# Inverse roots in two VectorE steps, with the logarithm reading the raw sum, and a last row tile in 512, 256, 128 and 128 columns

## The chip, the cores and the metric

The kernel runs on one core of one Trainium2 chip. The metric is device time in microseconds of one execution; lower is better. The core has a matmul engine (TensorE, PE in the profile, its weight loads PEld), VectorE (DVE), ScalarE (ACT), GpSimd (POOL) and SyncE (SP), which here issues all the DMAs.

## The reference

Four layers on 512 tokens of width 1024, all in float32. Layers 0 and 1 have four branches each (latent attention, stick-breaking attention, attention with forget gates, memory attention), gated and merged, an output projection, and a layer norm of `alpha * x + out`. Layers 2 and 3 begin with an RMS norm, have four other attentions (dense, windowed, neighbourhood, difference), gates and an output projection onto the residual. A last RMS norm with its own gain gives the result. What matters here:

```python
def _layer_norm(x, g, b):
    mu = mean(x); var = mean(square(x - mu))
    return (x - mu) * rsqrt(var + 1e-5) * g + b

def _rmsnorm(x, g):
    return x * rsqrt(mean(x * x) + 1e-6) * g
```

Inside the attentions there are RMS norms as well: of the two latents, of the dense attention's queries and keys per head, and of the difference attention's outputs per head.

## The kernel before

Every product is made of three matmuls (`mm3`, L324 to 330): each float32 operand is split into a high and a low part, and high x high, high x low and low x high are summed in PSUM. Each matmul loads its own stationary operand, 128 x 128. The weights stream in as 128 x 1024 tiles and are split by ScalarE (L319) and VectorE (L322). Activations lie with features on partitions (`zth`, `ztl`).

Inside a layer the parts are generators, and a string of words written out by hand (`ORDER1`, `ORDER2`) sets the order in which they are called. When the program is built, the tile framework fixes each engine's own order and the semaphores from that; so on VectorE one finds operations of the next row tile between those of one norm. The engines then run their queues in order.

A layer ends in `w_out` (L1123 to 1145). It takes the 512 tokens in four row tiles of 128. For each tile it makes the output projection in column pieces of 512 (`fs`), in each piece 8 blocks of 3 matmuls (layers 0 and 1) or 6 blocks of 3 (layers 2 and 3, where two more blocks were multiplied earlier into `early`). The last row tile of the last layer is made in pieces of 512, 256 and 256 columns. After each piece VectorE adds the residual part (L1142 or L1144) into `y`. Then `post` (in `end`) takes the whole row tile:

- layers 0 and 1: `ln_rows` (L1171 to 1184): statistics by `bn_stats`, the variance plus epsilon (L1177), `y - mean` times gain for both halves (L1180), the inverse root, and the product with it plus the bias (L1184);
- layers 1, 2 and 3: `rms_rows` (L1156 to 1169): for each piece ScalarE squares it and sums it along the row (L1162, two records: the square and the read of its sum), VectorE multiplies by the gain (L1163) and adds the sum, scaled, to the previous one (L1165); then the inverse root; then the first 512 columns are scaled by VectorE (L1168) and the other 512 by ScalarE (L1169);
- except at the end, `to_feature` (L1147 to 1154) transposes the tile on PE (L1153) in two groups of four blocks of 128 columns, and splits it into `zth` and `ztl` for the next layer. At the end two DMAs of SyncE store the two halves (L1234).

The inverse root is `rsqrt` (L344 to 354). For a column `v` it forms exp(-ln(v)/2) on ScalarE (L348, L349) and one Newton step with four operations on VectorE (L350 to L353):

```python
nc.vector.tensor_tensor(t, y, y, ALU.mult)
nc.vector.tensor_tensor(t, t, v, ALU.mult)
nc.vector.tensor_scalar(t, t, -0.5, 1.5, ALU.mult, ALU.add)
nc.vector.tensor_tensor(y, y, t, ALU.mult)
```

It is called on one column by `ln_rows` and `rms_rows` (20 calls), on 8 columns by `mla` (2) and `diff_d` (4), and on 24 columns by `dense_a` (2).

Of the kernel before, what the change touches and what calls it, by code (L numbers as in the profile page):

```python
# [9 lines left out]
F32 = mybir.dt.float32  # L10
# [3 lines left out]
AF = mybir.ActivationFunctionType  # L14
ALU = mybir.AluOpType
# [4 lines left out]
DM = 1024  # L20
DEPTH = 2
ALPHA = (2 * DEPTH) ** 0.25
LN_EPS = 1e-5
RMS_EPS = 1e-6
# [264 lines left out]
def cols(i, n=128):  # L289
    return slice(n * i, n * i + n)  # L290
# [20 lines left out]
class Build:  # L311
# [29 lines left out]
    def small(self, n, name="sm"):  # L341
        return self.smp.tile([128, n], F32, tag=f"sm{n}", name=name, bufs=12 if n == 1 else 8 if n == 16 else 3)

    def rsqrt(self, v):  # L344

        nc, n = self.nc, v.shape[1]
        y, t = self.small(n, "rs_y"), self.small(n, "rs_t")
        nc.scalar.activation(y, v, AF.Ln)  # L348
        nc.scalar.activation(y, y, AF.Exp, scale=-0.5)  # L349
        nc.vector.tensor_tensor(t, y, y, ALU.mult)  # L350
        nc.vector.tensor_tensor(t, t, v, ALU.mult)
        nc.vector.tensor_scalar(t, t, -0.5, 1.5, ALU.mult, ALU.add)
        nc.vector.tensor_tensor(y, y, t, ALU.mult)  # L353
        return y


    def w_prefetch(self, upto):
# [304 lines left out]
    def setup(self):  # L662
        nc, tc, ctx = self.nc, self.tc, self.ctx
        pool = lambda n, b, **k: ctx.enter_context(tc.tile_pool(name=n, bufs=b, **k))
        self.cp = pool("const", 1)
        self.psp, self.pss, self.pst, self.pso = (pool(n, b, space=PSUM) for n, b in zip(("psp", "pss", "pst", "pso"), BANKS))
        self.rawp, self.wp = pool("raw", RAW), pool("wp", WP)
        self.smp = pool("small", 8)
        self.w_done, self.w_ready, self.wout, self.stp = 0, {}, None, None
        self.xs = [nc.dram_tensor(f"xs{i}", (S, DM), F32).ap() for i in range(3)]  # L670
        ct = self.cp.tile([128, NCONST], F32, name="ct")
        self.c = {k: ct[:, o : o + n] for k, (o, n) in COFF.items()}
        self.ident = self.c["ident"]
        big = lambda nm: self.cp.tile([128, 8, S], F32R, name=nm)
        self.zth, self.ztl = big("zth"), big("ztl")
        self.zp, self.z = pool("z", ZO), {}
        self.gated = set()
        nc.scalar.preload_act_table_set(EXPS)
        with tc.tile_pool(name="x0", bufs=1) as xp:
            x = xp.tile([128, 2, 8, 256], F32, name="x0")  # L680
            at = 0
            for n, (hf, k0, k1) in enumerate(X0):
                v = x[:, hf, k0:k1]
                c = slice(at, at + 256 * (k1 - k0))
                at = c.stop
                nc.sync.dma_start(v, self.ins["xt"][:, c].rearrange("p (k t) -> p k t", t=256))
                if n in W0:
                    self.w_prefetch(W0[n])
                self.split(*(t[:, k0:k1, cols(hf, 256)] for t in (self.zth, self.ztl)), v)
        self.w_prefetch(WP)  # L690
        nc.sync.dma_start(ct, self.ins["const"])
# [226 lines left out]
    def mla(self, l):  # L918
        nc = self.nc
# [24 lines left out]
                craw.append(c)  # L944
        v8 = self.small(8, "v8")
        v8v = v8.rearrange("p (a b) -> p a b", b=2)
        nc.vector.tensor_scalar(v8v[:, :, 0], stat[:, :, 0, 0], 1.0 / 384, RMS_EPS, ALU.mult, ALU.add)
        nc.vector.tensor_scalar(v8v[:, :, 1], stat[:, :, 1, 0], 1.0 / 256, RMS_EPS, ALU.mult, ALU.add)
        rs = self.rsqrt(v8).rearrange("p (a b) -> p a b", b=2)
        qsc = self.kp.tile([128, 4, 2], F32, tag="qsc", name="qsc")  # L950
        nc.vector.tensor_scalar(qsc[:, :, 0], rs[:, :, 0], 96.0**-0.5, None, ALU.mult)
# [171 lines left out]
    def w_out(self, kind, l, lhs, post, last):  # L1123
        nc = self.nc
        ks = range(len(lhs[0]))
        for k in ks:
            self.w_get((kind, l, k))
        woh, wol = self.wout
        for tt in range(4):
            c = cols(tt)  # L1130
            y = self.bp.tile([128, DM], F32, tag="y", name="y", bufs=2)
            rows = self.resid_rows.get(tt) or [y[:, f] for f in (cols(0, 512), cols(1, 512))]
            if kind == "wo" and tt not in self.resid_rows:
                nc.sync.dma_start(y, self.resid[c])
            fs = [cols(0, 512), cols(1, 512)]
            if last and tt == 3:
                fs[1:] = [cols(2, 256), cols(3, 256)]
            for f in fs:
                ps = self.pss.tile([128, S], F32, tag="S", name="pso")[:, : f.stop - f.start]
                self.mm3(ps, [(lhs[0][k][:, c], lhs[1][k][:, c], woh[:, k, f], wol[:, k, f]) for k in ks])  # L1140
                if kind == "wo":
                    nc.vector.scalar_tensor_tensor(y[:, f], rows[f.start // 512], ALPHA, ps, ALU.mult, ALU.add)  # L1142
                else:
                    nc.vector.tensor_tensor(y[:, f], self.early[tt][f.start // 512][:, f.start % 512 :][:, : f.stop - f.start], ps, ALU.add)  # L1144
            post(tt, y, fs)
# [10 lines left out]
    def rms_rows(self, y, g, out, fs):  # L1156

        nc = self.nc
        v = None
        for f in fs:  # L1160
            junk, ss = self.pso.tile([128, S], F32, tag="O", name="junk"), self.small(1, "ss")
            nc.scalar.activation(junk[:, : f.stop - f.start], y[:, f], AF.Square, accum_out=ss)  # L1162
            nc.vector.tensor_tensor(out[:, f], y[:, f], g[:, f], ALU.mult)  # L1163
            v2 = self.small(1, "ssv")
            nc.vector.tensor_scalar(v2, ss, 1.0 / DM, RMS_EPS if v is None else v, ALU.mult, ALU.add)  # L1165
            v = v2
        rs = self.rsqrt(v)
        nc.vector.tensor_scalar(out[:, cols(0, 512)], out[:, cols(0, 512)], rs, None, ALU.mult)  # L1168
        nc.scalar.activation(out[:, cols(1, 512)], out[:, cols(1, 512)], AF.Copy, scale=rs)  # L1169

    def ln_rows(self, y, g, b):  # L1171
        nc = self.nc
        st, mv, v = self.small(12, "bn"), self.small(2, "mv"), self.small(1, "var")
        for hf in range(2):
            nc.vector.bn_stats(st[:, cols(hf, 6)], y[:, cols(hf, 512)])
        nc.vector.bn_aggr(mv, st.rearrange("p (a b) -> p a b", b=6))
        nc.vector.tensor_scalar(v, mv[:, 1:2], LN_EPS, None, ALU.add)  # L1177
        for hf in range(2):
            f = cols(hf, 512)
            nc.vector.scalar_tensor_tensor(y[:, f], y[:, f], mv[:, 0:1], g[hf], ALU.subtract, ALU.mult)  # L1180
        rs = self.rsqrt(v)
        for hf in range(2):
            f = cols(hf, 512)
            nc.vector.scalar_tensor_tensor(y[:, f], y[:, f], rs, b[hf], ALU.mult, ALU.add)  # L1184
# [32 lines left out]
    def end(self, L, kind, lhs, last):  # L1217

        nc, l = self.nc, L % 2
        gn = self.row(6 if L == 3 else 3 + L, "rmsg") if L == 3 or L in (1, 2) and not last else None  # L1220

        def post(tt, y, fs):
            c = cols(tt)
            if L < 2:
                self.ln_rows(y, self.lng, self.lnb)
            if not last:
                nc.sync.dma_start(self.xs[L][c], y)
            if gn is not None:
                n = self.bp.tile([128, DM], F32, tag="n", name="n")
                self.rms_rows(y, gn, n, fs)  # L1230
                y = n
            if last:
                for f in (cols(0, 512), cols(1, 512)):
                    nc.sync.dma_start(self.out[c, f], y[:, f])  # L1234
            else:
                self.to_feature(tt, y)

        self.w_out(kind, l, lhs, post, last)
# [48 lines left out]
    def dense_a(self, l):  # L1287
# [9 lines left out]
            self.rope(r, cos, sin)  # L1297
            raw.append(r if t == 2 else self.q_stack(r))
        v = self.small(24, "va")
        nc.vector.tensor_scalar(v, stat.rearrange("p a b c -> p (a b c)"), 1.0 / 64, RMS_EPS, ALU.mult, ALU.add)  # L1300
        rs = self.rsqrt(v)
        rs4 = rs.rearrange("p (a b c) -> p a b c", b=3, c=2)
        qsc = self.kp.tile([128, 24], F32, tag="qsc", name="qsc")
# [57 lines left out]
    def diff_d(self, l):  # L1361
# [34 lines left out]
        for pr in range(2):  # L1396
            ku = [unit(hl[2], cols(2 * pr + c, 32), (0, 1, 0, 1)) for c in range(2)]
            o, sm = self.new_o(), self.sums()
            for e in range(2):
# [17 lines left out]
                if e:  # L1417
                    sq = self.tmp("sqd")
                    nc.scalar.activation(sq, o, AF.Square)
                    stat = self.pst.tile([128, 4, 1, 2], F32, tag="T", name="statd")  # L1420
                    self.head_sums(stat, 0, sq)

                    rc, v = self.recip(sm), self.sums()
                    nc.vector.tensor_tensor(v, rc, rc, ALU.mult)
                    nc.vector.scalar_tensor_tensor(v, v, 1.0 / 64, stat.rearrange("p a b c -> p (b c) a"), ALU.mult, ALU.mult)
                    nc.vector.tensor_scalar(v, v, RMS_EPS, None, ALU.add)
                    rs = self.rsqrt(v.rearrange("p a b -> p (a b)")).rearrange("p (a b) -> p a b", a=2)
                    nc.vector.tensor_tensor(rc, rc, rs, ALU.mult)
                    self.finish(6 + pr, o, rc, g)
# [65 lines left out]
```

## Time and profile before

| | us |
|---|---|
| median of 3 runs (lowest, highest) | 1360.04 (1359.38, 1360.09) |
| the profiled execution | 1360.33 |
| its span, first to last instruction | 1358.2 |
| TensorE busy | 1328.5 (98%) |
| VectorE busy | 1000.3 (74%) |
| ScalarE busy | 811.3 (60%) |

The profile is of one execution. Times in its rows count from the first instruction; the execution's own time is 2.1 us longer than the span. A row says when an operation started, how long it took, its engine and line, what it writes and reads, and its shape. Matmuls are pipelined, and a record of one overlaps the next, so what a matmul costs in a stream is read from start to start. In square brackets at the end of a row stands for how long the engine had stood still and what released it.

### The profile page before, as it was taken

To read this page: it belongs to the slowest core of one execution; us is meant where nothing else is said; L and a number is where in the kernel's file an instruction comes from. 1 tells how busy PE (TensorE), PEld (TensorE's weight loads), DVE (VectorE), ACT (ScalarE), POOL (GpSimd) and SP (SyncE) were. 2 spreads that over 40 slices of the span, in tenths; PEclk is the share of its full clock that TensorE was granted. 3 is DMA by queue.
4 is the path that set the end of the run, shared out by engine and by line. 5 is a ranking of instruction groups with operands and counts; after the bars stand their busy time and mean duration, and the time that the engine had idled before them with its cause. 6 is when DMAs were issued, how large, how long until landed. Compare 5 with 4: busy or idle time off the path is not lost.

```text
span 1358.2 us, 20047 instructions
## 1 busy us (share of the span) xinstructions
PE 1328.5 (98%) x7096; PEld 1096.4 (81%) x7096; DVE 1000.3 (74%) x2075; ACT 811.3 (60%) x1662; POOL 4.4 (0%) x12
## 2 busy tenths in 40 slices
PE   7999999999999999999999999999999999999997
PEld 7887788777789777877777898788887888888876
DVE  6567547898863677378989876789787576797875
ACT  4585556765413775467856344776875435778763
POOL 0000000000000000000000000000000000000000
PEclk9999999999999999999999999999999999999999
DMA  7543322343524443233236246323454265225521
GB/s 230 178 129 95 102 70 78 94 125 111 181 78 137 150 118 102 78 85 90 90 102 203 107 125 176 107 78 83 106 171 149 102 171 157 78 54 135 154 77 65
DMA packets 62419, 160.32 MB, mean 118 GB/s; under 512 B 11184, under 2 KB 11824, under 8 KB 62320
## 3 DMA queue, kind: packets, MB, share of 16 engines
q1 hardware_dynamic: 62320, 159.05, 39.6%
q8 instruction: 56, 0.92, 0.3%
q14 instruction: 43, 0.35, 0.1%
HBM read 117.92 MB, written 8.91 MB: 93 GB/s over the span
## 4 chain that ended last, share of the span: by engine, by line
PE 85%; DVE 6%; ACT 5%; issue 2%; DMA 2%; SPq 0%; DVEq 0%; ACTq 0%
PE proj L329 12%; PE proj L328 12%; PE proj L330 12%; PE T L551 4%; PE pso L330 3%; PE pso L328 3%; PE pso L329 3%; PE O L557 3%; PE O L558 2%; PE projwb L329 2%; PE projwb L330 2%; PE projwb L328 2%; PE s L512 2%; PE s L908 2%; PE projv L329 2%; PE projv L328 2%
## 5 line engine op out<-in xcount | busy, mean ns | idle before, releaser
L328 PE MATMUL proj<-zth,wh 128*128 128x512 f32 (+1 forms) x864 | 321.5, 373 | 6.9 <-ACT wh L319 5.6
L330 PE MATMUL proj<-zth,wl 128*128 128x512 f32 (+1 forms) x864 | 322.2, 373 | 0.0
L329 PE MATMUL proj<-ztl,wh 128*128 128x512 f32 (+1 forms) x864 | 321.7, 372 | 0.2
L322 DVE TENSOR_TENSOR wl<-raw,wh 128x1024 fp32r<-128x1024 f32 (+3 forms) x153 | 182.9, 1196 | 111.3 <-ACT wh L319 109.5
L319 ACT CAST wh<-raw 128x1024 fp32r<-128x1024 f32 (+3 forms) x153 | 157.9, 1032 | 138.2 <-PE proj L329 106.3
L328 PEld LDWEIGHTS proj<-zth,wh 128*128 128x128 f32 x864 | 163.5, 189 | 30.0 <-ACT wh L319 5.6
L329 PEld LDWEIGHTS proj<-ztl,wh 128*128 128x128 f32 x864 | 163.7, 189 | 23.6 <-DVE ztl L322 0.7
L330 PEld LDWEIGHTS proj<-zth,wl 128*128 128x128 f32 x864 | 163.5, 189 | 23.0 <-DVE wl L322 0.2
L322 DVE TENSOR_TENSOR tl<-T,th 128x512 fp32r<-128x512 f32 (+3 forms) x176 | 100.2, 576 | 23.2 <-ACT th L319 21.6
L319 ACT CAST th<-T 128x512 fp32r<-128x512 f32 (+3 forms) x176 | 86.6, 499 | 34.8 <-PE T L551 32.5
L551 PE MATMUL T<-ct,p 128*128 128x128 f32 x560 | 87.9, 274 | 2.0 <-DVE o L640 1.2
L528 DVE TENSOR_REDUCE nm<-s 128x1 f32<-128x512 f32 (+1 forms) x128 | 77.1, 612 | 11.1 <-PE s L1405 6.0
L551 PEld LDWEIGHTS T<-ct,p 128*128 128x128 f32 x560 | 67.7, 140 | 16.8 <-DVE o L640 2.9
L534 ACT ACTIVATE p<-s,nm 128x512 f32<-128x512 f32 (+1 forms) x96 | 59.4, 622 | 19.5 <-DVE nm L528 18.8
L557 PE MATMUL O<-tl,V 128*128 128x512 f32 (+3 forms) x160 | 59.2, 371 | 0.9 <-DVE tl L322 0.2
L558 PE MATMUL O<-th,V 128*128 128x512 f32 (+3 forms) x160 | 55.4, 350 | 0.0
L329 PE MATMUL projv<-wl,zth 128*128 128x256 f32 (+1 forms) x192 | 54.4, 283 | 0.0
L328 PE MATMUL projv<-wh,zth 128*128 128x256 f32 (+1 forms) x192 | 54.3, 283 | 0.0
L330 PE MATMUL projv<-wh,ztl 128*128 128x256 f32 (+1 forms) x192 | 54.3, 283 | 0.0
L329 PE MATMUL projwb<-y,wh 128*128 128x512 f32 x128 | 51.5, 403 | 0.0
L330 PE MATMUL projwb<-y,wl 128*128 128x512 f32 x128 | 50.9, 398 | 0.0
L328 PE MATMUL projwb<-y,wh 128*128 128x512 f32 x128 | 50.9, 398 | 0.0
(378 smaller groups left out, 2877.3 us busy)
## 6 DMA issues: line engine op xcount, KB each, us to landing
raw<-in_w_dram SPq DMA_DIRECT2D x173, 512.0 KB
xs<-y SPq DMA_DIRECT2D x12, 512.0 KB
ks<-hs SPq DMA_DIRECT2D x32, 128.0 KB
early<-xs SPq DMA_DIRECT2D x16, 256.0 KB
bias<-in_bias_dram SPq DMA_DIRECT2D x8, 448.0 KB
qs<-hs SPq DMA_DIRECT2D x24, 128.0 KB
qs<-ls SPq DMA_DIRECT2D x24, 128.0 KB
hs<-ls SPq DMA_DIRECT2D x24, 128.0 KB
```

What stands on the lines that cost most here:

```text
L319: self.nc.scalar.copy(h, src)
L322: self.nc.vector.tensor_tensor(l, src, h, ALU.subtract)
L328: self.nc.tensor.matmul(ps, ah, bh, start=i == 0, stop=False)
L329: self.nc.tensor.matmul(ps, ah, bl, start=False, stop=False)
L330: self.nc.tensor.matmul(ps, al, bh, start=False, stop=i == n - 1)
L512: self.nc.tensor.matmul(s, q[:, cols(i)], k[:, k0 : k0 + w], start=True, stop=False)
L528: nc.vector.tensor_reduce(nm, s, AX.X, ALU.max, negate=True)
L534: nc.scalar.activation(p[:, :w], src, AF.Exp, bias=nm, scale=sc, accum_out=sm)
L551: nc.tensor.transpose(T[:, cols(a)], P[i][:, c : c + 128], self.ident)
L557: nc.tensor.matmul(o, vsel(j), tl[:, :w], start=j == 0, stop=False, skip_group_check=True)
L558: nc.tensor.matmul(o, vsel(j), th[:, :w], start=False, stop=j == nk - 1, skip_group_check=True)
L908: nc.tensor.matmul(z[:, c:w], m, x, start=False, stop=n == len(sums) - 1, skip_group_check=True)
```

## The change

`rsqrt` now takes four times the mean (`v4`), and optionally the raw source with a scale and a bias that ScalarE applies inside the logarithm: w = exp(-ln(4v)/2) is half the inverse root, and the Newton step becomes (3 - w * v4 * w) * w. On one column that is two VectorE operations, on more columns three. All callers scale their means and epsilons by 4. `rms_rows` passes the last sum of squares as the source, with the running sum of the earlier pieces as a per-row bias; the scaled total `v` is still made on VectorE for the Newton step. `ln_rows` passes the variance as the source and a constant column with four times epsilon as the bias; that column is written once at the start. `rms_rows` scales columns 0 to 639 on VectorE and 640 to 1023 on ScalarE, and the two stores at the end are cut there too. The last row tile of the last layer is made in pieces of 512, 256, 128 and 128 columns.

```diff
-    def rsqrt(self, v):
-
-        nc, n = self.nc, v.shape[1]
-        y, t = self.small(n, "rs_y"), self.small(n, "rs_t")
-        nc.scalar.activation(y, v, AF.Ln)
-        nc.scalar.activation(y, y, AF.Exp, scale=-0.5)
-        nc.vector.tensor_tensor(t, y, y, ALU.mult)
-        nc.vector.tensor_tensor(t, t, v, ALU.mult)
-        nc.vector.tensor_scalar(t, t, -0.5, 1.5, ALU.mult, ALU.add)
-        nc.vector.tensor_tensor(y, y, t, ALU.mult)
-        return y
+    def rsqrt(self, v4, src=None, scale=1.0, bias=0.0):
+
+
+        nc, n = self.nc, v4.shape[1]
+        w, t = self.small(n, "rs_w"), self.small(n, "rs_t")
+        nc.scalar.activation(w, v4 if src is None else src, AF.Ln, scale=scale, bias=bias)
+        nc.scalar.activation(w, w, AF.Exp, scale=-0.5)
+        if n == 1:
+            nc.vector.scalar_tensor_tensor(t, w, v4, w, ALU.mult, ALU.mult)
+        else:
+            nc.vector.tensor_tensor(t, w, w, ALU.mult)
+            nc.vector.tensor_tensor(t, t, v4, ALU.mult)
+        nc.vector.scalar_tensor_tensor(w, t, 3.0, w, ALU.subtract, ALU.mult, reverse0=True)
+        return w
...
+        self.eps4 = self.cp.tile([128, 1], F32, name="eps4")
+        nc.vector.memset(self.eps4, 4 * LN_EPS)
...
             if last and tt == 3:
-                fs[1:] = [cols(2, 256), cols(3, 256)]
+                fs[1:] = [cols(2, 256), cols(6), cols(7)]
...
             v2 = self.small(1, "ssv")
-            nc.vector.tensor_scalar(v2, ss, 1.0 / DM, RMS_EPS if v is None else v, ALU.mult, ALU.add)
+            old = 4 * RMS_EPS if v is None else v
+            nc.vector.tensor_scalar(v2, ss, 4.0 / DM, old, ALU.mult, ALU.add)
             v = v2
-        rs = self.rsqrt(v)
-        nc.vector.tensor_scalar(out[:, cols(0, 512)], out[:, cols(0, 512)], rs, None, ALU.mult)
-        nc.scalar.activation(out[:, cols(1, 512)], out[:, cols(1, 512)], AF.Copy, scale=rs)
+        rs = self.rsqrt(v, ss, 4.0 / DM, old)
+        a, b = slice(0, 640), slice(640, DM)
+        nc.vector.tensor_scalar(out[:, a], out[:, a], rs, None, ALU.mult)
+        nc.scalar.activation(out[:, b], out[:, b], AF.Copy, scale=rs)
...
-        nc.vector.tensor_scalar(v, mv[:, 1:2], LN_EPS, None, ALU.add)
+        nc.vector.tensor_scalar(v, mv[:, 1:2], 4.0, 4 * LN_EPS, ALU.mult, ALU.add)
...
-        rs = self.rsqrt(v)
+        rs = self.rsqrt(v, mv[:, 1:2], 4.0, self.eps4)
...
             if last:
-                for f in (cols(0, 512), cols(1, 512)):
+                for f in (slice(0, 640), slice(640, DM)):
                     nc.sync.dma_start(self.out[c, f], y[:, f])
```

In `mla`, `dense_a` and `diff_d` the means are scaled by 4 (for instance `4.0 / 384, 4 * RMS_EPS` for `1.0 / 384, RMS_EPS`), and nothing else is changed there.

## Rows read from the trace of the kernel before

**Rows 1.** The page's busy times: engine, busy us, share, instructions.

```profile
PE 1328.5 (98%) x7096; PEld 1096.4 (81%) x7096; DVE 1000.3 (74%) x2075; ACT 811.3 (60%) x1662; POOL 4.4 (0%) x12
```

**Rows 2.** Timeline of the end: start us, duration us, engine, line, operation, tiles.

```profile
1351.34 0.28 PE L330 MATMUL pso<-wout,y 128*128 128x256 f32 x1
1351.65 0.42 DVE L1144 TENSOR_TENSOR y<-early,pso 128x256 f32<-128x256 f32 x1 [0.65 <-PE pso L330]
...
1352.17 0.39 ACT L1162 ACTIVATE junk<-y 128x256 f32<-128x256 f32 x1 [1.62 <-DVE y L1144]
1352.49 0.19 ACT L1162 ACTIVATION_READ_ACCUMULATOR junk<-y 128x1 f32 x1
...
1352.96 0.20 ACT L348 ACTIVATE rs_y<-ssv 128x1 f32<-128x1 f32 x1 [0.28 <-DVE ssv L1165]
...
1353.43 0.16 DVE L350 TENSOR_TENSOR rs_t<-rs_y 128x1 f32<-128x1 f32 x1 [0.50 <-ACT rs_y L349]
...
1354.20 0.72 ACT L1169 ACTIVATE n<-n,rs_y 128x512 f32<-128x512 f32 x1 [0.81 <-DVE rs_y L353]
1354.20 0.48 DVE L1168 TENSOR_SCALAR n<-n,rs_y 128x512 f32<-128x512 f32 x1
```

**Rows 3.** Timeline of PE, matmuls of 256 and of 128 columns (128x128).

```profile
1347.20 0.28 PE L328 MATMUL pso<-wout,y 128*128 128x256 f32 x1
1347.32 0.28 PE L329 MATMUL pso<-wout,y 128*128 128x256 f32 x1
...
254.96 0.27 PE L557 MATMUL O<-tl,V 128*128 128x128 f32 x1
255.07 0.28 PE L558 MATMUL O<-th,V 128*128 128x128 f32 x1
...
271.62 0.23 PE L557 MATMUL O<-tl,V 128*128 128x128 f32 x1
271.68 0.27 PE L558 MATMUL O<-th,V 128*128 128x128 f32 x1
...
132.77 0.44 PE L908 MATMUL s<-sp,tri 128*128 128x128 f32 x2 [0.65 <-DVE sp L322]
```

**Rows 4.** Groups by line and shape: count, busy us, mean ns, idle before.

```profile
L1144 DVE TENSOR_TENSOR y<-early,pso 128x256 f32<-128x256 f32 x2 | 0.8, 421 | 1.1 <-PE pso L330 1.1
L1162 ACT ACTIVATE junk<-y 128x512 f32<-128x512 f32 x7 | 4.2, 600 | 8.9 <-DVE y L1144 8.9
L1162 ACT ACTIVATE junk<-y 128x256 f32<-128x256 f32 x2 | 0.8, 388 | 2.8 <-DVE y L1144 2.8
L898 DVE SCALAR_TENSOR_TENSOR zt<-s,zt 128x128 f32<-128x128 f32 x8 | 2.2, 278 | 0.2
```

**Rows 5.** The same view: pairs without and with a scalar from memory.

```profile
L1296 ACT ACTIVATE qa<-proj,cols 128x512 f32<-128x512 f32 x1 | 0.7, 682 | 0.0
L1294 ACT ACTIVATE sq<-proj 128x512 f32<-128x512 f32 x1 | 0.6, 593 | 0.0
...
L1165 DVE TENSOR_SCALAR ssv<-ss,ssv 128x1 f32<-128x1 f32 x5 | 1.1, 211 | 1.2 <-ACT junk L1162 1.0
L1165 DVE TENSOR_SCALAR ssv<-ss 128x1 f32<-128x1 f32 x4 | 0.6, 150 | 1.6 <-ACT junk L1162 1.6
```

**Rows 6.** SyncE's second store; the DMAs' rate in slices of 0.1 us from 1354.2.

```profile
1355.14 0.38 SPq L1234 DMA_DIRECT2D out_dram<-n  x1
...
GB/s 0 0 0 0 0 0 0 0 0 0 0 0 0 143 389 471 389 369 410 389 451 369 369 430 471 369 205 21 0 0 0 0 0 0 0 0 0 0 0 0
```

**Rows 7.** Waits of PE, whole run: total us, times, longest us.

```profile
PE projn L328 <- DVE ml L985: 2.6, 2, 1.3
...
PE Tx L1153 <- DVE n L1168: 1.0, 3, 0.4
...
PE Tx L1153 <- issue: 0.4, 2, 0.3
PE Tx L1153 <- DVE y L1184: 0.4, 2, 0.2
```

More of the change, by code (lines that the diff above doesn't have):

```diff
@@ L946, in mla @@
         v8v = v8.rearrange("p (a b) -> p a b", b=2)
-        nc.vector.tensor_scalar(v8v[:, :, 0], stat[:, :, 0, 0], 1.0 / 384, RMS_EPS, ALU.mult, ALU.add)
-        nc.vector.tensor_scalar(v8v[:, :, 1], stat[:, :, 1, 0], 1.0 / 256, RMS_EPS, ALU.mult, ALU.add)
+        nc.vector.tensor_scalar(v8v[:, :, 0], stat[:, :, 0, 0], 4.0 / 384, 4 * RMS_EPS, ALU.mult, ALU.add)
+        nc.vector.tensor_scalar(v8v[:, :, 1], stat[:, :, 1, 0], 4.0 / 256, 4 * RMS_EPS, ALU.mult, ALU.add)
         rs = self.rsqrt(v8).rearrange("p (a b) -> p a b", b=2)
@@ L1299, in dense_a @@
         v = self.small(24, "va")
-        nc.vector.tensor_scalar(v, stat.rearrange("p a b c -> p (a b c)"), 1.0 / 64, RMS_EPS, ALU.mult, ALU.add)
+        nc.vector.tensor_scalar(v, stat.rearrange("p a b c -> p (a b c)"), 4.0 / 64, 4 * RMS_EPS, ALU.mult, ALU.add)
         rs = self.rsqrt(v)
@@ L1424, in diff_d @@
                     nc.vector.tensor_tensor(v, rc, rc, ALU.mult)
-                    nc.vector.scalar_tensor_tensor(v, v, 1.0 / 64, stat.rearrange("p a b c -> p (b c) a"), ALU.mult, ALU.mult)
-                    nc.vector.tensor_scalar(v, v, RMS_EPS, None, ALU.add)
+                    nc.vector.scalar_tensor_tensor(v, v, 4.0 / 64, stat.rearrange("p a b c -> p (b c) a"), ALU.mult, ALU.mult)
+                    nc.vector.tensor_scalar(v, v, 4 * RMS_EPS, None, ALU.add)
                     rs = self.rsqrt(v.rearrange("p a b -> p (a b)")).rearrange("p (a b) -> p a b", a=2)
```

## The prediction

> **What bounds the kernel now.** I read the page's busy times first, then the chain of work that ended last, then the timeline of the last microseconds, then TensorE's waits over the whole run. TensorE (PE) is busy for 1328.5 of 1358.2 us [rows 1], so before the very end an operation of another engine counts only where PE stands still for it. After PE's last matmul nothing else is left to run beside, and there every step counts in full. The reader should see in [rows 2] one dependent line: last matmul at 1351.34, addition of the early part, square, read of the sum, scaled sum (L1165), logarithm, exponential, four small operations (the first is L350), the two halves of the scaling at 1354.20. Two stores follow [rows 6]. From the addition at 1351.65 to the end of the span that is 6.55 us.
>
> **Change, part 1: 128-column pieces.** The last 256 columns of the last row tile become two pieces of 128. A piece is 6 blocks of rows times 3 products, 18 matmuls, and each loads its weights anew. At 256 columns one follows the other after 0.12 us (1347.20, 1347.32; 0.1175 us over the piece) [rows 3]. For 128 columns this line has no row, but other lines do. In a chain with a new load each time the step is 0.11 (254.96 to 255.07) [rows 3]. A pair whose first load was done early, while PE worked on something else, steps by 0.06 (271.62 to 271.68). A pair that starts after a wait steps by about 0.16: its two records span 0.44 us, and one lasts 0.28 [rows 3]. I take 0.11, since 36 matmuls in a row are nearest to the chain. So 36 x 0.11 = 3.99 us (0.111 unrounded) stand in place of 18 x 0.1175 = 2.11: **PE ends 1.88 us later**. Half the columns cost nearly the same, as the step does not follow the column count below 256. The ends are 36 x 0.06 = 2.16 (+0.05) and 36 x 0.16 = 5.76 (+3.65).
>
> The Trainium skill, page "TensorE: Matmul & The Clock Gate", section "Back-to-back issue gap", gives about 81 ns for sustained pairs of load and matmul at 128 columns; the chain here shows 110. By that page the pieces would cost 36 x 0.081 - 2.11 = +0.81 us, an estimate from its figure, where the row gives +1.88.
>
> **Part 2: what the smaller piece saves behind it.** The addition takes 0.42 at 256 columns, and another two-input operation that reads matmul sums takes 0.28 at 128 (L898): -0.14. The square goes from 0.39 by the slope between 0.60 and 0.39, which is 0.105 per 128 columns: -0.11 [rows 4]. The extra round of addition, square, product and sum of the third piece (about 0.8 us of VectorE) runs beside the 2 us of PE for the fourth, so I cost it at nothing; if it were exposed it would cost those 0.8 us.
>
> **Part 3: the logarithm reads the sum itself.** Now the sum is read at 1352.49, VectorE scales it, and the logarithm starts at 1352.96, 0.47 later. Afterwards it starts right behind the read on its own engine: 0.19 for the read and about 0.03 to the next, as everywhere in this line. That is -0.25. But its bias is now a column in memory. The same engine's operation with such a column takes 682 ns against 593 without, on the same source [rows 5]: +0.09. Bounds are nothing and 0.12 (0.72 for the scaling against 0.60 for the square at 512 columns [rows 2, 4]). The scaled sum is still computed, on VectorE, while the exponential runs; it costs nothing as long as it is done before.
>
> **Part 4: two operations for four.** From 1353.43 to 1354.20 four operations take 0.77, about 0.19 each [rows 2]. The first of the new two takes a column as its scalar, which costs 211 against 150 ns in L1165 [rows 5]; with the step between operations that is 0.25, and the second is 0.19: 0.44, so -0.33 (bounds -0.25 and -0.38). The 8 calls on 8 or 24 columns lose one operation of 0.19. PE never waits on those calls [rows 7], so I count nothing; all eight exposed would give 1.5 us. The new constant is one small write before the first loads have landed: nothing, at most 0.15 (L1165's shorter form).
>
> **Part 5: 640 and 384 columns.** VectorE's half grows by 128 columns, from 0.48 by (0.48 - 0.15)/4 = +0.08; ScalarE's half shrinks from 0.72 to about 0.61. SyncE issues the first store after VectorE's half and the second only at 1355.14, behind the first issue, although ScalarE was done at 1354.92. And the data rate stands near 400 GB/s without a hole from 1355.5 to 1356.9, so the total sets the end, not the second store alone [rows 6]. The shorter ScalarE half is therefore worth nothing and the longer VectorE half costs: +0.08 (with 0 and +0.1 as ends).
>
> Sum of the end: +1.88 - 0.14 - 0.11 - 0.25 + 0.09 - 0.33 + 0.08 = **+1.22 us**.
>
> **Part 6: the other row tiles.** 20 calls on one column lie in the row tiles of four layers (8 in layer norms, 12 in RMS norms); 19 of them are not at the end. PE stands still before the transposes that follow them in seven places, 1.0 + 0.4 + 0.4 us, about 1.8 in all [rows 7]. A layer norm gets 0.33 shorter: its logarithm already hides under two 0.7 us operations. An RMS norm gets 0.25 - 0.09 + 0.33 - 0.08 = 0.41 shorter. Every one of the seven gaps is 0.4 or less, so if PE's order stays, nearly all go: -1.8. But the order of each engine is fixed when the program is built, by that builder's own estimate of durations. If it moves the transposes forward by as much as it thinks the norms got shorter, the gaps stay: 0. No row decides between them; I take the middle, **-0.9**. Behind a closed gap PE meets its next wait; the largest others that recur are 1.3 us, twice, before the key projections of the latent attention [rows 7], and the change does not touch what they wait for.
>
> Net: +1.22 - 0.9 = +0.3 us. The profiled execution took 1360.33 us, so the sum gives 1360.6; the median of the runs lies 0.29 lower, at 1360.04, and on that footing I predict **1360.3**. That is under 0.2% (2.7 us), about what a measurement of this kernel can tell from no change.
>
> **Rivals.**
> - *The weight loads hide.* If the 128-column matmuls step by 0.06, PE ends where it did (+0.05), the end is 0.61 shorter, and with all seven gaps gone the change gives 0.61 + 1.8 = 2.4: 1357.6. For it: such pairs exist. Against it: each comes behind a longer matmul or a wait, where the load had time; in the chain it is 0.11 [rows 3]. With half the gaps it is 1358.5. Chance 0.12. With its 81 ns the page of the Trainium skill named under part 1 lies between this rival and my forecast; by that figure the sum with half the gaps is +0.81 - 0.66 - 0.9, an estimate of 1359.3.
> - *Slower: the pieces step as after a wait.* At 0.16 PE ends 3.65 later; with the same -0.66 behind it and no gap closed that is +3.0: 1363.0. It is over the 2.7 us from a step of 0.152 on. For it: the pairs of 0.44 us. Against it: they follow a standstill, and here PE never stands. Chance 0.06. With the step I take and no gap closed the kernel is also slower, by 1.2 us (1361.3), but inside the band; that is part of my forecast's own range.
> - *The order moves elsewhere.* The change alters instructions from the first microseconds on, so the builder can place loads and casts anew anywhere. One wait of that size, 1.3 us [rows 7], gained or lost: 1359.0 or 1361.6; two of them, 1357.7 or 1362.9. Chance 0.17, to both sides alike.
> - *It does not do what it says.* For the wide calls there are three operations for four, not two; that is already counted at nothing.
>
> **How the numbers follow.** My forecast (the step near 0.11, gaps closed by none to all: 1359.5 to 1361.3) has 0.65. Range 1358.0 to 1362.2: it takes in the forecast's ends, one lost or won wait beside them, and most of the first rival. Faster by over 0.2% (under 1357.3) needs the hidden loads and a won wait together, or two or three won: 0.08. Slower by over 0.2% (over 1362.7): the second rival and part of the third: 0.08. Within: 0.84.
>
> **What would show it.** In the profile after: a step near 0.11 us between the 128-column matmuls of the last tile, and PE's last matmul 1.9 us later, less what the boundaries gave; the logarithm about 0.2 after the read of the sum starts and about 0.29 long; 0.45 from the first small operation to the scaling; the first store's issue about 0.6 after the scaling starts; about 5.9 us from the last addition to the end. At the seven transposes, gaps of nothing or of the same 0.2 to 0.4. I am wrong if the 128-column step is under 0.08 or over 0.15, or if a wait over 1 us has come or gone away from the norms.

## The result and the profile after

The changed kernel takes 1367.14 us (median of 5 runs, 1365.9 to 1368.34) against 1360.09 for the kernel before beside it (5 runs, 1359.38 to 1361.4): ratio 1.0051, 95% interval 1.004 to 1.0062. It is slower by about 7 us, outside the range of the prediction, and to its far side. The profiled execution took 1368.34 us.

The page's busy times come first, with the largest group of its costliest instructions.

```profile
span 1366.5 us, 20055 instructions
...
PE 1339.0 (98%) x7114; PEld 1101.9 (81%) x7114; DVE 997.8 (73%) x2031; ACT 814.9 (60%) x1664; POOL 4.4 (0%) x12
...
L328 PE MATMUL proj<-zth,wh 128*128 128x512 f32 (+1 forms) x864 | 323.2, 375 | 6.6 <-ACT wh L319 4.9
```

The span grew by 8.3 us, and TensorE's own busy time by 10.5 [rows 1], with only 18 more matmuls. So TensorE did not wait longer; it worked longer. The prediction looked at waits and at the end only.

The end is next: the timeline from the last matmul on, as in [rows 2].

```profile
1360.22 0.28 PE L330 MATMUL pso<-wout,y 128*128 128x128 f32 x1
...
1360.53 0.29 DVE L1149 TENSOR_TENSOR y<-early,pso 128x128 f32<-128x128 f32 x1 [0.98 <-PE pso L330]
...
1361.13 0.19 ACT L1167 ACTIVATION_READ_ACCUMULATOR junk<-y 128x1 f32 x1
1361.35 0.29 ACT L349 ACTIVATE rs_w<-ss,ssv 128x1 f32<-128x1 f32 x1
1361.35 0.21 DVE L1171 TENSOR_SCALAR ssv<-ss,ssv 128x1 f32<-128x1 f32 x1 [0.20 <-ACT junk L1167]
...
1361.91 0.22 DVE L352 SCALAR_TENSOR_TENSOR rs_t<-rs_w,ssv 128x1 f32<-128x1 f32 x1 [0.35 <-ACT rs_w L350]
1362.16 0.16 DVE L356 SCALAR_TENSOR_TENSOR rs_w<-rs_t,rs_w 128x1 f32<-128x1 f32 x1
...
1362.36 0.55 DVE L1175 TENSOR_SCALAR n<-n,rs_w 128x640 f32<-128x640 f32 x1
```

From the last addition to the scaling it is 1.83 us, where it was 2.55: 0.72 less, and the sum of parts 2 to 4 said 0.74. From the addition to the end of the span it is 1366.5 - 1360.53 = 5.97, where the prediction asked for about 5.9.

TensorE's waits over the run, in total, times and longest, as in [rows 7]. First two groups of the kernel before that [rows 7] leave out:

```profile
PE pso L328 <- ACT wout L319: 1.7, 2, 1.1
...
PE pse L328 <- DVE early L1264: 0.7, 2, 0.3
```

and now the kernel after:

```profile
PE projn L328 <- DVE ml L990: 2.6, 2, 1.3
...
PE pse L328 <- DVE early L1271: 1.1, 2, 0.6
...
PE pso L329 <- DVE wout L322: 0.8, 2, 0.4
...
PE Tx L1158 <- DVE n L1175: 0.5, 2, 0.3
...
PE Tx L1158 <- issue: 0.2, 1, 0.2
```

Before the transposes 0.7 us are left of 1.8. The output weights, for which TensorE waited 1.7 us in two waits before (the longest 1.1), now cost 0.8, and the early products rose from 0.7 to 1.1. Nothing here is longer by more than 0.5 us.

So the loss lies in the stream of matmuls itself. The next rows are the first and last of 58 projection matmuls of 512 columns that follow one another without a pause, and of 96 matmuls of 256 columns for the values, in the kernel before:

```profile
541.80 0.40 PE L330 MATMUL proj<-zth,wl 128*128 128x512 f32 x1
...
554.86 0.39 PE L330 MATMUL proj<-zth,wl 128*128 128x512 f32 x1
...
1112.07 0.28 PE L328 MATMUL projv<-wh,zth 128*128 128x256 f32 x1
...
1122.86 0.28 PE L330 MATMUL projv<-wh,ztl 128*128 128x256 f32 x1
```

and the same matmuls after:

```profile
544.16 0.40 PE L330 MATMUL proj<-zth,wl 128*128 128x512 f32 x1
...
557.46 0.40 PE L330 MATMUL proj<-zth,wl 128*128 128x512 f32 x1
...
1118.23 0.28 PE L328 MATMUL projv<-wh,zth 128*128 128x256 f32 x1
...
1129.47 0.28 PE L330 MATMUL projv<-wh,ztl 128*128 128x256 f32 x1
```

57 steps took 13.06 us and now take 13.30; 95 steps took 10.79 and now take 11.24. One step has grown from 229.1 to 233.3 ns, the other from 113.6 to 118.3, in code that the change does not touch. A single row cannot show that: the records last 0.39 or 0.40 in both.

What the change did touch is memory. The new constant `eps4` has 4 bytes per partition and takes 32, between the activations `zth`, `ztl` and the weights. In the compiled programs' addresses (the traces hold none) the activations stay, and the weights `wh`, `wl` and all that comes after them on that side, such as the merged activations `y` and `mr`, lie 32 bytes further on.

### The profile page after: what moved, and what is told of

Read it like the earlier page. It is cut to its first block, busy times and chain, and to the rows that moved or that the text cites. A ratio compares the mean times of both kernels' runs of the same rounds, so it can differ in the third digit from the quotient of the medians.

```text
span 1366.5 us, 20055 instructions
## 1 busy us (share of the span) xinstructions
PE 1339.0 (98%) x7114; PEld 1101.9 (81%) x7114; DVE 997.8 (73%) x2031; ACT 814.9 (60%) x1664; POOL 4.4 (0%) x12
## 4 chain that ended last, share of the span: by engine, by line
PE 87%; DVE 5%; ACT 4%; DMA 3%; issue 1%; SPq 0%; DVEq 0%; ACTq 0%
PE proj L328 12%; PE proj L330 12%; PE proj L329 12%; PE T L554 4%; PE pso L328 3%; PE pso L330 3%; PE pso L329 3%; PE O L560 3%; PE O L561 2%; PE projwb L329 2%; PE projwb L330 2%; PE projwb L328 2%; PE s L515 2%; PE projv L330 2%; PE projv L328 2%; PE s L913 2%
```

## The experiments

The theory: the step of a matmul depends on where its two operands lie to each other, and the 32 bytes changed that. The rivals: another order of the engines, or the change's own operations.

**The column alone.** The kernel before with only the column.

```diff
-        self.gated = set()
+        self.gated, self.eps4 = set(), self.cp.tile([128, 1], F32, name="eps4"); nc.vector.memset(self.eps4, 4 * LN_EPS)
```

> The kernel before, with nothing added but the change's constant column of 4 bytes per partition and the small write that fills it; nobody reads it. In the program that comes out the column takes 32 bytes, and what is placed behind it in the same region of SBUF (the weight tiles wh and wl, the gates, the score operands) lies 32 bytes further on, while zth, ztl and the tiles of the other region stay. Every engine's order is that of before. Placement theory: the matmuls of the projections read weights and activations whose places have shifted against each other, and step by 233 instead of 230 ns at 512 columns, so this kernel is as slow as the changed one's projections make it: 1365 to 1367 us. Order theory (the new order of the engines costs the 7 us): 1360 us, as before, with steps of 230 ns. Tail theory (pieces of 128 columns): 1360 us.

Measured: 1367.42 us (6 runs), ratio 1.0047 (1.0034 to 1.0059). The same 58 matmuls:

```profile
543.37 0.40 PE L330 MATMUL proj<-zth,wl 128*128 128x512 f32 x1
...
556.67 0.40 PE L330 MATMUL proj<-zth,wl 128*128 128x512 f32 x1
```

13.30 us, as after. A column that nobody reads costs as much as the whole change; the rivals fall. The size is less certain: three of the six runs have a mean granted clock of TensorE of 0.996 (the last section shows what takes it down), which none of the 29 runs of the kernel before beside them has. At 0.998 it is 1366.4 us (2 runs) against 1360.1 (12 runs): 6.3 more.

**64 bytes.** The changed kernel with a column out of a tile of 64 bytes, so that the weights move by 64 from where they lay before.

```diff
-        self.eps4 = self.cp.tile([128, 1], F32, name="eps4")
+        self.eps4 = self.cp.tile([128, 16], F32, name="eps4")[:, 0:1]
```

> The changed kernel with its constant column as the first of a tile of 64 bytes per partition, so that the weight tiles lie 64 bytes further on than before, not 32. Every engine's order is that of the changed kernel. Placement theory: projection steps of 230 ns again, 6 us less than the changed kernel: 1360.5 to 1362 us. Order theory: 1367 us, unchanged. Tail theory: 1367 us.

Measured: 1363.43 us (11 runs), ratio 1.0024 (1.0015 to 1.0032): half of the loss is gone, less than expected. The rows tell why.

```profile
540.80 0.40 PE L330 MATMUL proj<-zth,wl 128*128 128x512 f32 x1
...
553.77 0.39 PE L330 MATMUL proj<-zth,wl 128*128 128x512 f32 x1
...
1112.31 0.28 PE L328 MATMUL projv<-wh,zth 128*128 128x256 f32 x1
...
1123.70 0.28 PE L330 MATMUL projv<-wh,ztl 128*128 128x256 f32 x1
```

The 58 matmuls take 12.97 us, less than before. But the 96 of 256 columns take 11.39, more than after. One placement can serve one kind of matmul and hurt another.

**The column first.** The changed kernel with the column ahead of `zth`, so that activations and weights both move by 32 bytes and keep their distance.

```diff
+        self.eps4 = self.cp.tile([128, 1], F32, name="eps4")
         big = lambda nm: self.cp.tile([128, 8, S], F32R, name=nm)
         self.zth, self.ztl = big("zth"), big("ztl")
         self.zp, self.z = pool("z", ZO), {}
         self.gated = set()
-        self.eps4 = self.cp.tile([128, 1], F32, name="eps4")
```

> The changed kernel with its constant column placed ahead of zth and ztl, so that these move by 32 bytes as the weight tiles do, and their distance is that of before again. Matmul order unchanged. If the distance of the two operands decides: projection steps of 230 ns, and instead the output projections of layers 0 and 1, whose weights lie in the other region, rise from 229 to 233 (384 matmuls, 1.5 us): 1362 to 1363 us. If the weight tiles' own place decides: like the changed kernel, 1367 us. Order theory: 1367 us.

Measured: 1363.21 us (11 runs), ratio 1.002 (1.0011 to 1.0029). The projections are back at 230.0 ns. The output projections that read `zth` have gone from 229.2 to 233.2: the output weights lie at the other end of the memory and did not move. So it is the distance that counts, not the address of one operand.

**64 bytes and 256 columns.** The 64-byte kernel with the last row tile in the old pieces.

```diff
-                fs[1:] = [cols(2, 256), cols(6), cols(7)]
+                fs[1:] = [cols(2, 256), cols(3, 256)]
```

> As the 64-byte version of the changed kernel, but the last row tile ends in pieces of 512, 256 and 256 columns as before. By the prediction's sum TensorE ends 1.88 us earlier and the line behind it is 0.25 us longer: 1.6 us less than the 64-byte version (1359 to 1360 us by the placement theory). Rival, weight loads hidden at 128 columns: 0.25 us more than the 64-byte version. With the pieces of 128 columns as the cause of the 7 us: 1360 us while the 64-byte version stays at 1367.

Measured: 1362.67 us (11 runs), ratio 1.0017 (1.0008 to 1.0025): 0.8 less, not 1.6. The direction is right, the size was open until the later runs.

**The column among the constants.** The changed kernel at the placement of before: the column becomes the last one of the constants that are loaded anyway, in bytes that were padding.

```diff
-    c["sgn"] = np.where((p % 32) < 16, -1.0, 1.0)[:, None]
+    c["sgn"], c["eps4"] = np.where((p % 32) < 16, -1.0, 1.0)[:, None], 4 * LN_EPS * np.ones((128, 1))
...
-        self.eps4 = self.cp.tile([128, 1], F32, name="eps4")
-        nc.vector.memset(self.eps4, 4 * LN_EPS)
...
-        rs = self.rsqrt(v, mv[:, 1:2], 4.0, self.eps4)
+        rs = self.rsqrt(v, mv[:, 1:2], 4.0, self.c["eps4"])
```

> The changed kernel, with four times epsilon as one more column of the constants that are loaded anyway. All tiles lie where they lie in the kernel before; the order of every engine is that of the changed kernel, without the one write of the column. Placement theory: the steps go back to those of the kernel before (512 columns 230 ns, values 113 to 114 ns), and the time is that of before, 1360.0 us, + 1.2 for the end and - 1.0 for the shorter waits before the transposes: 1360.2 us (1359.4 to 1361.0). Rival, the change's own operations and order cost something beside the placement: over 1362 us.

Measured: 1360.63 us (11 runs) against 1360.3 for the kernel before (33 runs): ratio 1.0003 (0.9994 to 1.0012).

```profile
541.70 0.39 PE L330 MATMUL proj<-zth,wl 128*128 128x512 f32 x1
...
554.76 0.39 PE L330 MATMUL proj<-zth,wl 128*128 128x512 f32 x1
```

13.06 us again, to the digit of before. Within that interval all of the loss was placement; the change without it is worth +0.3 us by the medians (-0.8 to +1.6 by the interval), and the sum of the prediction had said +0.3.

**The same with 256 columns.** The edit is that of the fourth run, on the kernel just above.

> The same, with the last row tile in pieces of 512, 256 and 256 as before. If the 128-column pieces cost what the sum of the end says (+1.88 for the matmuls, -0.25 behind them), 1.6 us less than the run with the column in the constants: 1358.6 us. If they cost half of that, as the earlier pair of runs with 64 bytes read (0.8 us): 1359.4 us. If they are free: 1360.2 us.

Measured: 1359.53 us (11 runs), ratio 0.9994 (0.9985 to 1.0003). The pieces cost 1.1 us here, between the two estimates.

**The pieces of 128 columns alone,** on the kernel before:

```diff
-                fs[1:] = [cols(2, 256), cols(3, 256)]
+                fs[1:] = [cols(2, 256), cols(6), cols(7)]
```

> The kernel before with only the pieces of the last row tile changed, to 512, 256, 128 and 128. Placement is untouched. By the sum: +1.88 for 36 matmuls at 0.111 us in place of 18 at 0.1175, -0.25 for the shorter addition and square: 1360.0 + 1.6 = 1361.6 us. If the smaller piece gives back all it costs: 1360.0 us.

Measured: 1362.15 us (11 runs), ratio 1.0012 (1.0003 to 1.0021), 1.85 more than before. The timeline shows the first matmul of the 256-column piece, the first of 128 columns and the last.

```profile
1347.63 0.28 PE L328 MATMUL pso<-wout,y 128*128 128x256 f32 x1
...
1349.75 0.23 PE L328 MATMUL pso<-wout,y 128*128 128x128 f32 x1
...
1353.61 0.28 PE L330 MATMUL pso<-wout,y 128*128 128x128 f32 x1
```

35 steps take 3.86 us: 0.110 each. From the first row to the last it is 5.98, where two pieces of 256 columns took 1351.34 - 1347.20 = 4.14: 1.84 more, and the prediction said 1.88. Behind it, addition to scaling takes 2.31 instead of 2.55: -0.24, and the prediction said -0.25. With 1.88 for the matmuls the run with 256 columns ought to have gained 1.6 and gained 1.1. The last slices of its transfers (the DMAs' rate in 40 slices from 1352.8 to 1357.9) hold the rest.

```profile
GB/s 0 0 0 0 0 0 0 0 0 0 0 0 20 422 381 361 361 462 402 346 438 361 361 177 12 12 24 24 12 0 0 0 0 0 0 0 0 0 0 0
...
q14 instruction: 1, 0.01, 0.4%
```

A load of code falls among the two stores, and after the main part some 12 to 24 GB/s trickle on for 0.6 us. From the scaling to the end it takes about 4.75 us, where after has 4.14. All four kernels that have the new inverse root and 256-column pieces have such a load among their stores and show 4.7 to 4.8; the eight others have none there and show 4.0 to 4.2. That the load of code delays the last packets is read from these rows and not shown; moving it was not tried.

**160 bytes between.** Two runs with an unused tile of 160 bytes between the weights and what follows, which moves `y` and `mr` only. No instruction is added.

```diff
-        self.smp = pool("small", 8)
+        self.pad, self.smp = pool("pad", 1).tile([128, 40], F32, name="pad"), pool("small", 8)
```

On the kernel with the column among the constants and 256-column pieces:

> The same as the run before it (constants, 256), with an unused tile of 160 bytes per partition between the weights and the small tiles; no instruction is added and every engine's order is the same. It moves the merged activations by 160 bytes, so that they lie at the same distance (192 modulo 256 bytes) from the weights as the projections' operands do, which step by 230 ns. If the distance sets the step, 560 matmuls of the gates and merges fall from 234.2 to about 230 (-2.4 us) and 265 of the output projection from 233.2 to about 229.5 (-1.0): 3.4 us less than the run before it, about 1355.2 us. If the pattern is only that of the projections: no difference, 1358.6 us.

Measured: 1357.71 us (11 runs), ratio 0.9985 (0.9976 to 0.9994). It beats both kernels; but it is 1.8 less than without the tile, where 3.4 were expected. Gates and merges in the run without the tile, the first and last of 149 matmuls without a pause:

```profile
684.43 0.40 PE L329 MATMUL projmu<-mr,wh 128*128 128x512 f32 x1
...
719.11 0.40 PE L330 MATMUL projmu<-mr,wl 128*128 128x512 f32 x1
```

With the tile, the first and the 75th, and the weight load behind it:

```profile
682.69 0.41 PE L328 MATMUL projmu<-mr,wh 128*128 128x512 f32 x1
...
699.65 0.40 PE L329 MATMUL projwb<-y,wh 128*128 128x512 f32 x1
...
699.80 0.19 PEld L330 LDWEIGHTS projwb<-y,wl 128*128 128x128 f32 x1 [0.18 <-DVE wl L322]
```

34.68 us over 148 steps is 234.3 ns; 16.96 over 74 is 229.2. The steps are as expected, and they are shorter by 4.7 in 520 of 576 matmuls here and by 3.7 in 240 of the output projection (the table below), 3.3 us together. The stream without a pause is now broken, because TensorE arrives ahead of VectorE's split of the weights. VectorE is busy for 36 of 40 us in this stretch (680 to 720). From the first matmul of the gates and merges to the last it takes 73.4 and 73.2 us in the two layers without the tile, and 72.6 in both with it. That is 1.4 less, where the shorter steps alone would give 2.4; the other 1.0 went into longer pauses, of which the new wait for VectorE is one. What is left of the missing 1.5 us is open.

The medians of these two kernels also differ in the granted clock. With the tile, six runs at a clock of 0.999 take 1357.05 to 1357.7 us and five at 0.996 take 1359.0 to 1360.24; without it, all eleven lie at 0.997 or 0.998. So the 1.8 is not placement alone; by the two ratios (0.9985 and 0.9994) the tile is worth 1.2.

On the kernel before, with nothing else changed:

> The kernel before, nothing changed but the unused tile of 160 bytes per partition; no instruction is added and every engine's order is that of before. If the gain of the run with the constants, 256-column pieces and 160 bytes is all from placement, the gates and merges fall from 234.2 to about 229.5 ns and the time is 1.8 us under that of before: about 1358.4 us. If the tile's worth depends on the change, no difference from before (1360.2 us).

Measured: 1358.46 us (11 runs), ratio 0.9987 (0.9979 to 0.9996). Here the gain also stands at equal clock: at 0.999 it is 1357.4 us (6 runs) against 1358.9 (3 runs). So about 1.7 us are to be had without the change, and most of the gain of the kernel above is from placement, not from the inverse roots.

**32 bytes between,** the tile of 40 columns cut to 8:

> The run with the constants and 256-column pieces, with an unused tile of 32 bytes per partition where the other had 160. The merged activations then lie 64 bytes (modulo 256) from the weights, and the output projection's pair 64 too; the starts of both operands agree modulo 64. If what counts is agreement modulo 64, the gates and merges step by 230 ns as in the run with 160 bytes, and the time is about 1357.7 us. If what counts is the distance modulo 256, at which 0 and 192 have been fast and 32, 64, 96, 160 and 224 slow, they stay at 233 to 234 ns and the time is that without the tile, about 1359.5 us.

Measured: 1360.09 us (10 runs), ratio 0.9997 (0.9987 to 1.0006).

```profile
684.74 0.39 PE L329 MATMUL projmu<-mr,wh 128*128 128x512 f32 x1
...
719.27 0.40 PE L330 MATMUL projmu<-mr,wl 128*128 128x512 f32 x1
```

34.53 us, 233.3 ns. Starts that agree modulo 64 are not enough.

The table puts the runs together. Each entry is a distance and a step. The distance is the start of the stationary operand that is being loaded less the start of the moving operand of the matmul that runs meanwhile, modulo 256 bytes, from the compiled addresses. The step is the mean in ns from start to start in the trace, over pairs of the same kind, without those behind a pause. The kernels left out have the placement of one that is shown.

| kernel | projections, 512 | gates and merges, 512 | output from `zth`, 512 | output from `y`, 512 | projections, 256 | values, 256 |
|---|---|---|---|---|---|---|
| matmuls | 2016 | 576 | 384 | 270 | 576 | 384 |
| before | 192: 229.9 | 96: 234.2 | 192: 229.5 | 32: 233.2 | 192: 116.8 | 64: 113.6 |
| after | 224: 232.9 | 96: 234.3 | 192: 229.2 | 64: 233.4 | 224: 116.7 | 32: 118.3 |
| column alone | 224: 232.9 | 96: 234.2 | 192: 229.3 | 64: 233.3 | 224: 116.9 | 32: 118.3 |
| 64 bytes | 0: 229.0 | 96: 234.2 | 192: 229.2 | 96: 234.1 | 0: 119.9 | 0: 119.9 |
| column first | 192: 230.0 | 96: 234.2 | 224: 233.2 | 64: 233.2 | 192: 117.8 | 64: 114.6 |
| among the constants | 192: 229.8 | 96: 234.1 | 192: 229.2 | 32: 233.0 | 192: 117.2 | 64: 114.6 |
| and 256, 160 bytes | 192: 230.0 | 192: 229.5 | 192: 229.1 | 192: 229.4 | 192: 117.8 | 64: 114.6 |
| and 256, 32 bytes | 192: 230.0 | 64: 233.3 | 192: 229.8 | 64: 233.3 | 192: 117.8 | 64: 114.6 |
| before, 160 bytes | 192: 230.1 | 192: 229.4 | 192: 229.2 | 192: 229.7 | 192: 117.8 | 64: 113.6 |

At 512 columns distances of 0 and 192 give 229 to 230 ns and 32, 64, 96 and 224 give 233 to 234, whichever the tiles. At 256 columns 64 is the best (114) and 0 the worst (120). The last row tile's own pieces of 256 columns, which are not in the table, agree: 113.7 ns in the kernel with 32 bytes, where their distance is 64, and 117.4 to 118.2 in the six other kernels that have two of them. A difference of 1 ns at 256 columns says nothing about distance: the values at 64 take 113.6 in the kernels with the old inverse root and 114.6 in those with the new one, and the reason is open.

## Why the prediction was wrong

**The step that failed** is the last sentence of part 4: "The new constant is one small write before the first loads have landed: nothing, at most 0.15". Nothing shows the write to cost anything. Its 32 bytes cost 6 to 7 us: about 1594 projection steps in unbroken streams at +3.0 ns are 4.8 us, 380 of the values at +4.7 are 1.8, together 6.6, and if the projections outside such streams paid it too, 7.9. The column alone measured 7.4 by the medians (6.4 by the ratio). I priced the instruction and not the memory it takes, and I bounded the cost of that edit by rows for instructions, none of which could have shown it.

The rest of the sum held. The column among the constants gives the change at the old placement: 1360.63 where the text said 1360.3, and +0.3 to the kernel beside it where the sum said +0.3. That the two agree to the digit is luck, as the interval runs from -0.8 to +1.6. By its parts:

- *Part 1.* The chain of 128-column matmuls was the right row: 0.110 us, +1.84 for +1.88. The Trainium skill's page "TensorE: Matmul & The Clock Gate", section "Back-to-back issue gap", gives 81 ns for such pairs; by the 0.110 of these 36 in a row the measurement decides against it here.
- *Parts 2, 3 and 4.* 0.24 for 0.25, and 0.49 for 0.49 (2.55 to 2.06 in the runs with the new root and 256-column pieces). The logarithm starts 0.22 after the read of the sum starts and lasts 0.29, as asked.
- *Part 5.* From scaling to end +0.14 for +0.08. That a load of code can lie among the stores was not seen.
- *Part 6.* 1.1 of the 1.8 us before the transposes went, for the 0.9 taken. The new order also took 0.9 from the waits for the output weights and gave 0.4 to those for the early products. All standstills of TensorE together fell by 0.9 (17.5 to 16.6 us): the forecast number, but reached by other waits than the transposes alone, and so in part luck too.

None of the rivals explains the loss. The hidden loads and the 0.16 step are refuted by the 0.110; the order did shorten the waits for the output weights (the longest from 1.1 to 0.4 us, which the prediction had named as a sign of being wrong), but that is a gain. Of what would show the prediction, one thing plainly failed: TensorE's last matmul starts at 1360.22 us and not at 1351.34, 8.9 later where 1.9 at most was asked. All three rivals, and the rest of that list, spoke of waits and of the end, and there nearly all came as asked. None asked whether the 7000 other matmuls would keep their step. With TensorE at 98% that was the largest term of all: 1 ns on each of 2016 matmuls is 2 us, as much as the dearest edit of the diff.

The two profiled executions differ by 8.0 us. The steps (6.6), the end (5.91 - 4.14 for the pieces of the last tile, -0.58 behind them: 1.2), TensorE's standstills (17.5 us before, 16.6 after: -0.9) and one more stretch at the lower clock (below, 1.2) make 8.1, so about 1.2 of the 8.0 us belong to a stretch that not every execution has.

## What to carry to other kernels

Where TensorE streams matmuls that each load their weights, compare the mean step over a long unbroken stream before and after any edit that allocates memory, even 4 bytes; the single record's duration does not show it. When a step has changed in code that was not touched, look at where the tiles lie before looking for a reason in the order. New small constants go where they displace nothing, into the padding of a tile that exists, and a few bytes of unused space in the right place can be worth more than a tuned chain of operations.

## What the runs showed of the hardware beyond that

That the step depends on the distance was unexpected. The Trainium skill's page "SBUF — State Buffer", section "SBUF: two separate sides", says that TensorE's ports wait for no other engine. The loss here does not speak against that: the column alone gave VectorE one instruction more (2075 to 2076) and the other engines none. What in the memory makes the distance count was not measured, only that the step goes with it at each of the distances in the table.

The granted clock had a second surprise. Right after the two standstills of 1.3 us before the key projections, some executions run 3.4 us at the lower level, and others do not. The windows around the first of them, in the kernel after (us, busy time and count of PE, PEld, DVE, ACT and POOL, clock, DMA share, GB/s):

```profile
250.00:253.50 3.50, 3.50 (x10) 2.73 (x11) 2.71 (x5) 1.60 (x4) 0.00 (x0) 0.53 0.34 81
253.50:257.00 3.50, 3.50 (x22) 2.99 (x21) 2.40 (x7) 2.04 (x4) 0.00 (x0) 0.99 0.18 9
```

and in the run with 64 bytes:

```profile
248.50:252.00 3.50, 3.50 (x23) 3.23 (x23) 3.08 (x5) 2.39 (x5) 0.00 (x0) 1.00 0.19 47
```

At 1.2 GHz 10 matmuls begin in the time of 22. What such a stretch costs is read at the second place, which ran at the full clock in the kernel before and had a stretch in the kernel after. From the matmul that ends the standstill to the same one 44 matmuls later, before:

```profile
635.40 0.51 PE L328 MATMUL projn<-ckh,wh 128*128 128x512 f32 x1 [1.29 <-DVE ml L985]
...
643.57 0.40 PE L328 MATMUL projn<-cqh,wh 128*128 128x512 f32 x1
```

and after:

```profile
638.77 0.50 PE L328 MATMUL projn<-ckh,wh 128*128 128x512 f32 x1 [1.30 <-DVE ml L990]
...
648.12 0.40 PE L328 MATMUL projn<-cqh,wh 128*128 128x512 f32 x1
```

8.17 us against 9.35: 1.2 lost. The profile before had one such stretch, after had two, the 64-byte run none, with the same standstills in all. This goes some way to explain why the runs of one kernel lie some us apart; what decides it is open.
